# Attention in pairs of units, pinned on TensorE, with another order of branches, in a two-layer mixer step

## The chip, the cores and the metric

The kernel runs on one core of a Trainium2 chip. The metric is the device time of one execution in microseconds: the median of three runs, and beside it one execution that the hardware profiler recorded.

## What is computed

Two layers of a decoder step, for a prompt of 1024 tokens and 8 sample tokens (one new token for each of 8 sequences), model width 1024. Each layer projects the normalised input once and splits it among four branches of width 384, gates and projects them, merges them, and adds the result to the residual. Cut to what matters here:

```python
h = rms_norm(x, norm_g)
(a_b, a_c, a_h, a_gate, s_q, s_k, s_v, s_gate,
 c_u, c_v, c_gate, d_q, d_k, d_v, d_gate) = jnp.split(h @ w_in, SPLIT_POINTS, axis=-1)
y_a = a_b * conv3(a_c * a_h)                                    # A
o_b, _ = banded_window_attention(q, k, v, SWA_WINDOW, sink)     # B: 6 q heads, 2 kv heads, window 128
y_c = c_u * chunk_spatial_mix(vn, w_spatial, b_spatial)         # C
for g, (win, dil) in enumerate(((128, 1), (512, 4), (2048, 16))):
    o, lse = dilated_prompt_attention(qg, kg, vg, win, dil)     # D: 2 heads a group, blocks of 128
y_d = concat(o * softmax(lse over groups))
proj_b = einsum('bsne,ned->bsnd', [y_n * silu(gate_n)], w_branch)
x = x + sum(sigmoid(h @ w_merge) * proj_b) @ w_out
```

Attention works on blocks of 128 queries against at most 256 keys. The updated caches are outputs too.

## The kernel before, in words

Activations lie transposed in SBUF: 128 features on the partitions, 1032 token columns (8 sample tokens, then 1024). `slot` gives a tile of that size from a pool of 31. Every weight and every activation of a dense product is split into a high and a low fp32r part (`split_w`: ScalarE rounds to the high part, L154, GpSimd subtracts, L156), and a product is three matmuls for each 128 input features: high weight by high activation (L178), high by low (L181), low by high (L182), in chunks of 344 columns (`fm_tile`, `mm_cols`). The accumulators are `acc` tiles, one PSUM bank each. `tm_group` (L367 to L371) does the same with tokens on the partitions. These are called dense matmuls here.

Attention is cut into units: one block of 128 queries of two heads (one from each half of the partitions), against `nk` = 128 or 256 keys. Branch B has 24 units in a layer (8 blocks, 3 pairs of heads), branch D has 8 in each of 3 groups: 48 in a layer. For one unit, before:

- `scores` (L519): a matmul for each head, contraction over 64 partitions, into one `sc` bank each; VectorE scales, masks and takes the maximum (L521);
- `exps` (L527, ScalarE); in B the sum, its reciprocal and the scaling follow on VectorE (L568 to L576);
- `pv`: transpositions of the weights (L536) into an `ms` bank, a copy to SBUF on ScalarE (L538), and the matmuls with the values (L541) into another `ms` bank, which ScalarE copies out.

PSUM has 8 banks: 4 for `acc`, 2 for `sc`, 2 for `ms`.

The order on each engine isn't that of the source: a scheduler takes the instructions in the source's order of priority, by its own forecast of when each can start, and fills TensorE with whatever it holds to be ready. A few edges (`load`'s "prefetch distance") order DMAs behind matmuls. On the chip each engine keeps to the order built.

The branches come in this order: keys, queries and values of B; C's values; C's products, with B's units among them; then `conv_a(0, branch_d(0))`, decode of group 0 and of B, `gate_a(0)`, B's gates, `conv_a(1, branch_d(1))`, `gate_a(1)`, `conv_a(2, branch_d(2))`, the gate of group 0, the end of D's decode, `gate_a(2)`, and the merge. `branch_d(g)` projects and rotates one group's keys and queries (`rope`: a half swap by DMA, then VectorE and GpSimd, L289 to L297) and runs its 8 units. At the start `x` is transposed on TensorE (L259, L262) into `sc` and `ms` banks in turn, copied by VectorE (L264) and split (L207 to L214).

Of the kernel before, what the change touches and what calls it, by code (L numbers as in the profile page):

```python
# [7 lines left out]
F32 = mybir.dt.float32  # L8
F32R = mybir.dt.float32r
AF = mybir.ActivationFunctionType  # L10
ALU = mybir.AluOpType
# [21 lines left out]
def kernel(ctx: ExitStack, tc: tile.TileContext, i, o, c):  # L33
# [5 lines left out]
    sl = ctx.enter_context(tc.tile_pool(name="sl", bufs=31))  # L39
# [21 lines left out]
    def pscore():  # L61
        return psS.tile([P, 512], F32, tag="sc", name="sc")
# [188 lines left out]
    for n0, n1 in GROUPS:  # L251
# [22 lines left out]
    for l in range(2):  # L274
# [239 lines left out]
        def scores(qs, ks, nk, mask, mx):  # L514

            s = tp.tile([P, 2, 256], F32, tag="s", name="s", bufs=2)
            ps = [pscore() for _ in range(2)]
            for h in range(2):
                pe.matmul(ps[h][:, :nk], qs[h], ks[h], start=True, stop=True)  # L519
            for h in range(2):  # L520
                dve.tensor_tensor_reduce(s[:, h, :nk], ps[h][:, :nk], mask, scale=0.125,  # L521
                                         scalar=-3e38, op0=ALU.add, op1=ALU.max, accum_out=mx[:, h:h + 1])
            return s

        def exps(s, nk, negm, den):
            for h in range(2):
                act.activation(s[:, h, :nk], s[:, h, :nk], AF.Exp, bias=negm[:, h:h + 1],  # L527
                               accum_out=den[:, h:h + 1])

        def pv(s, nk, vs, out):  # L530

            kb = nk // P
            ps = pmisc()
            for h in range(2):
                for b in range(kb):
                    pe.transpose(ps[:, (h * kb + b) * P:(h * kb + b + 1) * P], s[:, h, b * P:(b + 1) * P], ident)  # L536
            pt = tp.tile([P, 512], F32, tag="pt", name="pt")
            act.activation(pt[:, :2 * nk], ps[:, :2 * nk], AF.Copy)  # L538
            for b in range(kb):
                for h in range(2):  # L540
                    pe.matmul(out[h * 64:(h + 1) * 64, :], vs[b][h], pt[:, (h * kb + b) * P:(h * kb + b + 1) * P],  # L541
                              start=(b == 0), stop=(b == kb - 1))
# [15 lines left out]
        stB = sm.tile([P, 8, 3, 4], F32, tag="stB", name="stB")  # L558
        for n in range(8):
# [3 lines left out]
            ks = halves(kB, (slice(None), kcols))  # L563
            for j in range(3):
                st = stB[:, n, j]
                s = scores(halves(qB[j], (slice(None), blkcols(n))), ks, nk, mask, st[:, 0:2])
                negm = st[:, 0:2]
                dve.scalar_tensor_tensor(negm, st[:, 0:2], -1.0, nsink[:, j], op0=ALU.mult, op1=ALU.min)  # L568
                exps(s, nk, negm, st[:, 2:4])
                es = sm.tile([P, 2], F32, tag="es", name="es", bufs=4)  # L570
                dve.tensor_tensor(es, negm, nsink[:, j], op=ALU.subtract)
                act.activation(es, es, AF.Exp)
                dve.tensor_tensor(es, es, st[:, 2:4], op=ALU.add)
                dve.reciprocal(es, es)
                for h in range(2):
                    dve.tensor_scalar(s[:, h, :nk], s[:, h, :nk], es[:, h:h + 1], None, op0=ALU.mult)  # L576
                kbs = (n - 1, n) if n else (n,)
                vs = [[vB[:, b, h * 64:(h + 1) * 64] for h in range(2)] for b in kbs]
                po = pmisc()
                pv(s, nk, vs, po[:, :P])  # L580
                act.activation(OB[j][:, blkcols(n)], po[:, :P], AF.Copy)
# [131 lines left out]
        def conv_a(j, rows):  # L713
# [7 lines left out]
            rows()  # L721
# [24 lines left out]
        def gate_a(j):  # L746
            y = yA[j]
            fm_tile(w_std(win_cols(l, A_B + P * j, P), KT), KT, hh, hl, ev_mul(y))
            fm_tile(w_std(win_cols(l, A_G + P * j, P), KT), KT, hh, hl, ev_silu(y))
            store_later(1, yscr[0][j], y)  # L750
# [4 lines left out]
        def branch_d(g):  # L755
# [8 lines left out]
            for nm, src, lst in (("dqs", dq, dqs), ("dks", dk, dks)):  # L764
                t = sm.tile([P, NS], F32, tag=f"{nm}{g}", name=f"{nm}{g}")
                dve.tensor_copy(t, src[:, 0:NS])
                lst.append(t)
            vg = load_v(1 + g)
# [3 lines left out]
            std = sm.tile([P, 8, 4], F32, tag="std", name="std")  # L772
            for u in range(8):
# [25 lines left out]
                s = scores(qv, kv_, nk, mask, std[:, u, 0:2])  # L799
                negm = sm.tile([P, 2], F32, tag="es", name="negm", bufs=4)  # L800
                dve.tensor_scalar(negm, std[:, u, 0:2], -1.0, None, op0=ALU.mult)
                exps(s, nk, negm, std[:, u, 2:4])
                po = pmisc()
# [273 lines left out]
```

## Time and profile before

| | |
|---|---|
| median of 3 runs | 2435.44 us (2435.28 to 2436.69) |
| the profiled execution, its own time | 2441.25 us |
| its span, first to last instruction | 2439.3 us |
| TensorE busy (matmul) | 2418.7 us, 99% |
| TensorE's weight loader busy | 2303.7 us, 94% |
| VectorE, ScalarE, GpSimd busy | 910.6, 703.4, 842.8 us |
| mean granted TensorE clock | 0.992 |
| chain that ended last | TensorE 95%, VectorE 2%, DMA 1%, ScalarE 1% |

TensorE has two rows: PE is matmuls, PEld is the loading of the stationary operand, which runs beside them. A matmul of two full fp32 operands (S and R here) appears as two records, a transposition or a dense fp32r matmul as one. A matmul's duration overlaps its successor's; the distance between two starts is what one costs.

### The profile page before, as it was taken

The page shows a single profiled execution, that of the slowest core. Times are in us where ns is not written, and L with a number is a line of the kernel's source. Part 1 is how long each engine was busy: PE and PEld are TensorE (multiplying, and loading weights), DVE is VectorE, ACT ScalarE, POOL GpSimd, SP SyncE. Part 2 cuts the span into 40 slices and gives each one's busy share as a digit, 9 for nine tenths or more (in the row PEclk, how much of TensorE's full clock was granted, in tenths as well). Part 3 has the DMA queues.
Part 4 walks back from the last instruction along what each step waited for, and adds up shares of the span by engine and source line. Part 5 has one row for each costly group of instructions (what it writes and reads, how often), then busy time and mean ns, then how long its engine had stood idle before and what let it go on. Part 6 is the DMA issues. An engine that isn't in the chain of part 4 may idle for free.

```text
span 2439.3 us, 38864 instructions
## 1 busy us (share of the span) xinstructions
PE 2418.7 (99%) x15896; PEld 2303.7 (94%) x15896; DVE 910.6 (37%) x1938; ACT 703.4 (29%) x1526; POOL 842.8 (35%) x556
## 2 busy tenths in 40 slices
PE   8999999999999999999999999999999999999999
PEld 7998889899999999999999888898999999999998
DVE  4456526354312221225323554443353221212253
ACT  6234432323212221214323253313222222222243
POOL 3342225342223343334433313342323234434330
PEclk9999999999899999999999999999999999999999
DMA  7252224343322222224443413242352222212232
GB/s 241 87 145 82 74 57 151 87 125 94 102 70 63 88 62 96 65 65 129 140 146 82 151 53 96 80 148 57 100 143 71 70 92 65 88 61 69 76 98 99
DMA packets 295962, 235.82 MB, mean 97 GB/s; under 512 B 52756, under 2 KB 279696, under 8 KB 293416
## 3 DMA queue, kind: packets, MB, share of 16 engines
q1 hardware_dynamic: 267952, 206.25, 28.1%
q10 hardware_dynamic: 27832, 27.10, 3.9%
q8 instruction: 125, 2.05, 0.4%
q14 instruction: 53, 0.43, 0.1%
HBM read 192.35 MB, written 76.47 MB: 110 GB/s over the span
## 4 chain that ended last, share of the span: by engine, by line
PE 95%; DVE 2%; DMA 1%; ACT 1%; ACTq 0%; issue 0%; POOL 0%; SPq 0%; DVEq 0%; POOLq 0%
PE acc L181 26%; PE acc L178 26%; PE acc L182 26%; PE sc L519 2%; PE acc L367 2%; PE acc L370 2%; PE acc L371 2%; PE ms L541 2%; PE ms L536 2%; PE ms L681 1%; DVE ml L901 0%; DMA wr<-in_w_in_dram 0%; PE ms L474 0%; ACT wh L154 0%; DMA qs<-dq 0%
## 5 line engine op out<-in xcount | busy, mean ns | idle before, releaser
L156 POOL TENSOR_TENSOR wl<-wr,wh 128x384 fp32r<-128x384 f32 (+2 forms) x228 | 462.7, 2031 | 925.5 <-ACT wh L154 796.8
L178 PE MATMUL acc<-h0h,wh 128*128 128x344 f32 x1584 | 513.4, 324 | 1.9 <-ACT wh L154 0.9
L178 PE MATMUL acc<-h1h,wh 128*128 128x344 f32 x1584 | 514.4, 325 | 0.9 <-ACT dk L281 0.5
L181 PE MATMUL acc<-h1l,wh 128*128 128x344 f32 x1584 | 513.5, 324 | 0.0
L181 PE MATMUL acc<-h0l,wh 128*128 128x344 f32 x1584 | 512.8, 324 | 0.0
L182 PE MATMUL acc<-h0h,wl 128*128 128x344 f32 x1584 | 512.5, 324 | 0.0
L182 PE MATMUL acc<-h1h,wl 128*128 128x344 f32 x1584 | 510.8, 323 | 0.0
L154 ACT ACTIVATE wh<-wr 128x384 fp32r<-128x384 f32 (+2 forms) x228 | 205.2, 901 | 457.4 <-PE acc L181 422.8
L936 DVE TENSOR_TENSOR th<-acc,rr 128x344 f32<-128x344 f32 x192 | 99.0, 516 | 565.9 <-PE acc L182 562.3
L181 PEld LDWEIGHTS acc<-h0l,wh 128*128 128x128 f32 x1584 | 300.3, 190 | 8.7 <-issue 7.6
L181 PEld LDWEIGHTS acc<-h1l,wh 128*128 128x128 f32 x1584 | 300.2, 190 | 8.3 <-issue 7.6
L178 PEld LDWEIGHTS acc<-h0h,wh 128*128 128x128 f32 x1584 | 300.1, 190 | 7.4 <-issue 2.7
L178 PEld LDWEIGHTS acc<-h1h,wh 128*128 128x128 f32 x1584 | 299.9, 189 | 5.8 <-issue 2.9
L182 PEld LDWEIGHTS acc<-h1h,wl 128*128 128x128 f32 x1584 | 300.4, 190 | 2.8 <-issue 1.8
L182 PEld LDWEIGHTS acc<-h0h,wl 128*128 128x128 f32 x1584 | 299.9, 189 | 2.8 <-issue 1.8
L942 POOL TENSOR_TENSOR mg<-mg,th 128x344 f32<-128x344 f32 x144 | 138.0, 958 | 308.4 <-DVE th L941 308.4
L937 ACT ACTIVATE th<-th 128x344 f32<-128x344 f32 x192 | 94.3, 491 | 520.9 <-DVE th L936 520.9
L178 PE MATMUL acc<-yh,wh 128*128 128x344 f32 x576 | 184.5, 320 | 0.0
L181 PE MATMUL acc<-yl,wh 128*128 128x344 f32 x576 | 184.0, 319 | 0.0
L182 PE MATMUL acc<-yh,wl 128*128 128x344 f32 x576 | 183.8, 319 | 0.0
L181 PE MATMUL acc<-ml,wh 128*128 128x344 f32 (+3 forms) x384 | 123.2, 322 | 0.5 <-DVE ml L901 0.5
L941 DVE SCALAR_TENSOR_TENSOR th<-th,acc 128x344 f32<-128x344 f32 x144 | 73.8, 512 | 130.2 <-PE acc L182 129.5
(280 smaller groups left out, 3363.9 us busy)
## 6 DMA issues: line engine op xcount, KB each, us to landing
wr<-in_w_merge_dram SPq DMA_DIRECT2D x64, 512.0 KB
out_dram<-in_cache_dil_kv_dram SPq DMA_DIRECT2D x128, 255.9 KB
wr<-in_w_in_dram SPq DMA_DIRECT2D x60, 512.0 KB
y<-yscr SPq DMA_DIRECT2D x18, 516.0 KB
wr<-in_w_branch_dram SPq DMA_DIRECT2D x48, 192.0 KB
wr<-in_w_in_dram SPq DMA_DIRECT2D x32, 256.0 KB
wr<-in_w_out_dram SPq DMA_DIRECT2D x16, 512.0 KB
out_dram<-in_cache_dil_kv_dram SPq DMA_DIRECT2D x16, 511.0 KB
```

Of the source, the lines that this page charges most:

```text
L154: act.activation(hi, raw, AF.Copy)
L156: pool.tensor_tensor(lo, raw, hi.bitcast(F32), op=ALU.subtract)
L178: mm = pe.matmul(ps[:, :n], hi[:, k], xh[k][:, cs], start=(k == 0), stop=False)
L181: pe.matmul(ps[:, :n], hi[:, k], xl[k][:, cs], start=False, stop=False)
L182: pe.matmul(ps[:, :n], lo[:, k], xh[k][:, cs], start=False, stop=(k == kt - 1))
L367: mm = pe.matmul(ps[:M, :N], lh, hi[:, k % kk], start=(k == 0), stop=False)
L370: pe.matmul(ps[:M, :N], ll, hi[:, k % kk], start=False, stop=False)
L371: pe.matmul(ps[:M, :N], lh, lo[:, k % kk], start=False, stop=(k == KT - 1))
L936: dve.tensor_tensor(t, pg[:, :CH], rr[:, cs], op=ALU.mult)
L937: act.activation(t, t, AF.Tanh, scale=0.5)
L941: dve.scalar_tensor_tensor(t, t, 1.0, pp[:, :CH], op0=ALU.add, op1=ALU.mult)
L942: pool.tensor_tensor(mg[m][:, cs], mg[m][:, cs], t, op=ALU.add)
```

## The change

The units of one attention are collected in a list, and `attend` works through them two at a time:

- `psS` becomes one tile of two banks, head by bank, which holds the scores of two units side by side; `psM` gets 3 banks, `psA` 3 instead of 4. Users of `sc` for other things take `acc` (input) or `ms` (final block).
- For a pair, the source issues on TensorE: its transpositions, then the results of the pair before, then the scores of the next pair. `pin` orders each of these behind the TensorE instruction that the source issued just before it (an order of issue, not a wait).
- `conv_a` no longer contains a branch D; `gate_a` is split into `in_a` (the product with A_B) and `out_a` (the gate); `branch_d` returns two functions, one for the cache rows and one for the attention, and the order of the calls changes.
- The pool of slots grows from 31 to 34.

```diff
-    sl = ctx.enter_context(tc.tile_pool(name="sl", bufs=31))
+    sl = ctx.enter_context(tc.tile_pool(name="sl", bufs=34))
...
-    psA = ctx.enter_context(tc.tile_pool(name="psA", bufs=4, space=bass.MemoryType.PSUM))
-    psS = ctx.enter_context(tc.tile_pool(name="psS", bufs=2, space=bass.MemoryType.PSUM))
-    psM = ctx.enter_context(tc.tile_pool(name="psM", bufs=2, space=bass.MemoryType.PSUM))
+    psA = ctx.enter_context(tc.tile_pool(name="psA", bufs=3, space=bass.MemoryType.PSUM))
+    psS = ctx.enter_context(tc.tile_pool(name="psS", bufs=1, space=bass.MemoryType.PSUM))
+    psM = ctx.enter_context(tc.tile_pool(name="psM", bufs=3, space=bass.MemoryType.PSUM))
...
-        return psS.tile([P, 512], F32, tag="sc", name="sc")
+        return psS.tile([P, 2, 512], F32, tag="sc", name="sc")
...
-            ps = pmisc() if k % 2 else pscore()
+            ps = pmisc() if k % 2 else pacc()
...
+        def attend(units):
+            pinned = [False]
+            def pin(ins):
+                if pinned[0]:
+                    tc.keep_in_program_order(ins)
+                pinned[0] = True
+            def scores(pair):
+                ps = pscore()
+                for a, u in enumerate(pair):
+                    for h in range(2):
+                        pin(pe.matmul(ps[:, h, a * 256:a * 256 + u.nk], u.qs[h], u.ks[h], start=True, stop=True))
+                return ps
...
+            def transposed(pair):
+                for u in reversed(pair):
+                    kb = u.nk // P
+                    ps = pmisc()
+                    for h in (1, 0):
+                        for b in range(kb):
+                            pin(pe.transpose(ps[:, (h * kb + b) * P:(h * kb + b + 1) * P],
+                                             u.s[:, h, b * P:(b + 1) * P], ident))
+                    u.pt = tp.tile([P, 512], F32, tag="pt", name="pt")
+                    act.activation(u.pt[:, :2 * u.nk], ps[:, :2 * u.nk], AF.Copy)
+            def results(pair):
+                po = pmisc()
+                for a, u in enumerate(pair):
+                    kb = u.nk // P
+                    for b in range(kb):
+                        for h in range(2):
+                            pin(pe.matmul(po[h * 64:(h + 1) * 64, a * P:(a + 1) * P], u.vs[b][h],
+                                          u.pt[:, (h * kb + b) * P:(h * kb + b + 1) * P],
+                                          start=(b == 0), stop=(b == kb - 1)))
+                for a, u in enumerate(pair):
+                    act.activation(u.out, po[:, a * P:(a + 1) * P], AF.Copy)
+            pairs = [units[n:n + 2] for n in range(0, len(units), 2)]
+            ps = scores(pairs[0])
+            for n, pair in enumerate(pairs):
+                soften(pair, ps)
+                pinned[0] = False
+                transposed(pair)
+                if n:
+                    results(pairs[n - 1])
+                if n + 1 < len(pairs):
+                    ps = scores(pairs[n + 1])
+            pinned[0] = False
+            results(pairs[-1])
...
         decD = Decode("D")
-        conv_a(0, branch_d(0))
+        rows, attention = branch_d(0)
+        conv_a(0, rows)
         decD.scores(0, dqs[0], dks[0])
+        attention()
+        in_a(0)
+        conv_a(1)
...
-        gate_a(0)
+        out_a(0)
...
-        conv_a(1, branch_d(1))
+        rows, attention = branch_d(1)
+        in_a(1)
+        rows()
         decD.scores(1, dqs[1], dks[1])
-        gate_a(1)
-        conv_a(2, branch_d(2))
+        attention()
+        out_a(1)
+        conv_a(2)
+        rows, attention = branch_d(2)
+        sg0 = gate_d(0)
+        rows()
         decD.scores(2, dqs[2], dks[2])
-        sg0 = gate_d(0)
+        attention()
+        in_a(2)
...
-        gate_a(2)
+        out_a(2)
```

`soften` holds the masked maximum of `scores` for both units and then each unit's softmax, unchanged in its operations.

How the built order moves, first on TensorE in B's attention of the first layer, in the middle of it. `v` are the values, `s` the weights, `kB` and `qB` keys and queries; the dense rows are C's products. Before:

```order
L178 MATMUL acc<-h0h_133,wh 128x344
L541 MATMUL ms<-pt,v_1753 64x128 x4
L536 MATMUL ms<-ident,s 128x128 x4
L519 MATMUL sc<-kB,qB_863 128x256 x2
L181 MATMUL acc<-h0l_141,wh 128x344
L182 MATMUL acc<-h0h_133,wl 128x344
```

And with the change:

```order
L178 MATMUL acc<-h0h_133,wh 128x344
L553 MATMUL ms<-ident,s 128x128 x8
L564 MATMUL ms<-pt,v_1753 64x128 x8
L535 MATMUL sc<-kB,qB_1242 128x256 x2
L535 MATMUL sc<-kB,qB_359 128x256 x2
L181 MATMUL acc<-h0l_141,wh 128x344
L182 MATMUL acc<-h0h_133,wl 128x344
```

The first kind of group stands after every 18 dense matmuls, the second after every 57 to 64, with twice the attention in it and the transpositions ahead.

Second on TensorE at the start of the program, where `xin` is the input that arrives by DMA. Before, dense matmuls stand among the transpositions from the 29th row on:

```order
L262 MATMUL sc<-ident,xin_97 128x128
L262 MATMUL sc<-ident,xin_101 128x128
L262 MATMUL sc<-ident,xin_103 128x128
L178 MATMUL acc<-h0h_128,wh 128x344
L181 MATMUL acc<-h0l_136,wh 128x344
L259 MATMUL ms<-ident,xs 128x8
L262 MATMUL ms<-ident,xin_97 128x128
```

With the change the first dense matmul is the 69th row, behind transpositions of the last two input blocks:

```order
L262 MATMUL acc<-ident,xin_120 128x128
L262 MATMUL acc<-ident,xin_122 128x128
L262 MATMUL ms<-ident,xin_120 128x128
L262 MATMUL ms<-ident,xin_122 128x128
L178 MATMUL acc<-h0h_128,wh 128x344
L181 MATMUL acc<-h0l_136,wh 128x344
```

The transpositions write `acc` and `ms` tiles there instead of `sc` and `ms`.

## Rows read from the trace of the kernel before

**Rows 1.** The page, its first part: busy us (share of the span) xinstructions by engine.

```profile
PE 2418.7 (99%) x15896; PEld 2303.7 (94%) x15896; DVE 910.6 (37%) x1938; ACT 703.4 (29%) x1526; POOL 842.8 (35%) x556
```

**Rows 2.** Waits of TensorE's matmuls: line, released by: us in total, times, longest.

```profile
PE sc L259 <- DMA xs<-in_x_sample_dram: 4.6, 1, 4.6
PE sc L519 <- DVE dqp L297: 3.6, 3, 3.2
PE ms L259 <- DVE xT L264: 2.4, 1, 2.4
```

**Rows 3.** Waits of TensorE's weight loader, same columns.

```profile
PEld ms L541 <- issue: 18.9, 87, 0.3
PEld sc L519 <- issue: 17.0, 91, 0.3
PEld acc L181 <- issue: 15.3, 48, 0.3
PEld ms L536 <- issue: 15.1, 88, 0.2
```

**Rows 4.** Timeline of TensorE in B's attention: start us, us, operation, xcount.

```profile
251.70 0.32 PE L182 MATMUL acc<-h0h,wl 128*128 128x344 f32 x1
251.85 0.32 PE L178 MATMUL acc<-h0h,wh 128*128 128x344 f32 x1
252.10 0.66 PE L541 MATMUL ms<-pt,v 128*64 128x128 f32 x8
252.69 0.66 PE L536 MATMUL ms<-ident,s 128*128 128x128 f32 x4
253.28 0.70 PE L519 MATMUL sc<-kB,qB 64*128 64x256 f32 x4
253.91 0.42 PE L181 MATMUL acc<-h0l,wh 128*128 128x344 f32 x1
254.17 0.32 PE L182 MATMUL acc<-h0h,wl 128*128 128x344 f32 x1
```

**Rows 5.** Timeline of TensorE near the end: transpositions among dense matmuls.

```profile
2415.61 0.34 PE L178 MATMUL acc<-mh,wh 128*128 128x384 f32 x1
2415.78 1.03 PE L973 MATMUL sc<-ident,xT 128*128 128x128 f32 x8
...
2416.84 0.35 PE L182 MATMUL acc<-mh,wl 128*128 128x384 f32 x1
```

**Rows 6.** Timeline of TensorE in D's first group: results of a short unit.

```profile
328.80 0.44 PE L541 MATMUL ms<-pt,v 128*64 128x128 f32 x4
```

**Rows 7.** Start: records on `acc` to 28.3 us by engine, and two dense starts.

```profile
0.00:28.30 28.30, 9.19 (x33) 6.70 (x34) 0.00 (x0) 0.00 (x0) 1.00 0.78 216
18.45 0.49 PE L178 MATMUL acc<-h0h,wh 128*128 128x344 f32 x1
18.74 0.49 PE L181 MATMUL acc<-h0l,wh 128*128 128x344 f32 x1
```

**Rows 8.** Timeline of VectorE at the start; in brackets its wait and what ended it.

```profile
8.46 0.57 DVE L264 COPY xT<-sc 128x392 f32<-128x392 f32 x1 [7.50 <-PE sc L262]
10.73 0.55 DVE L264 COPY xT<-sc 128x392 f32<-128x392 f32 x1
14.43 2.30 DVE L209 SCALAR_TENSOR_TENSOR h0l<-xT,gcol,h0h 128x392 fp32r<-128x392 f32 x1 [3.14 <-ACT h0h L207]
```

**Rows 9.** Timeline of VectorE in B's attention: the scaling of one unit's weights.

```profile
256.72 0.61 DVE L576 TENSOR_SCALAR s<-s,es 128x256 f32<-128x256 f32 x2
```

**Rows 10.** TensorE before a fall; stretches: us, PE busy (x), granted clock, DMA.

```profile
418.04 1.09 PE L681 MATMUL ms<-pd,cB 128*64 128x3 f32 x16
420.40:423.80 3.40, 3.40 (x14) 0.50 0.78 310
467.60:471.20 3.60, 3.60 (x21) 1.00 0.47 135
2430.90:2437.70 6.80, 3.08 (x26) 1.00 0.63 233
```

More of the change, by code (lines that the diff above doesn't have):

```diff
@@ L511, in cache_k @@
             act.dma_start(dst, kr)
-        def scores(qs, ks, nk, mask, mx):
-            s = tp.tile([P, 2, 256], F32, tag="s", name="s", bufs=2)
-            ps = [pscore() for _ in range(2)]
-            for h in range(2):
[L519 to L542, printed above, removed]
+        class Unit:
+            def __init__(self, qs, ks, nk, mask, vs, mx, den, soft, out):
+                self.qs, self.ks, self.nk, self.mask, self.vs = qs, ks, nk, mask, vs
+                self.mx, self.den, self.soft, self.out = mx, den, soft, out
@@ L544, in halves, with exps @@
+        def exps(u, negm):
+            for h in range(2):
+                act.activation(u.s[:, h, :u.nk], u.s[:, h, :u.nk], AF.Exp, bias=negm[:, h:h + 1],
+                               accum_out=u.den[:, h:h + 1])
         def halves(t, sel):
@@ L558 @@
         stB = sm.tile([P, 8, 3, 4], F32, tag="stB", name="stB")
+        units = []
         for n in range(8):
@@ L563, with soft @@
             ks = halves(kB, (slice(None), kcols))
+            kbs = (n - 1, n) if n else (n,)
+            vs = [[vB[:, b, h * 64:(h + 1) * 64] for h in range(2)] for b in kbs]
             for j in range(3):
-                st = stB[:, n, j]
[L566 to L581, printed above, removed]
+                def soft(u, j=j):
+                    negm = u.mx
+                    dve.scalar_tensor_tensor(negm, u.mx, -1.0, nsink[:, j], op0=ALU.mult, op1=ALU.min)
+                    exps(u, negm)
+                    es = sm.tile([P, 2], F32, tag="es", name="es", bufs=4)
+                    dve.tensor_tensor(es, negm, nsink[:, j], op=ALU.subtract)
+                    act.activation(es, es, AF.Exp)
+                    dve.tensor_tensor(es, es, u.den, op=ALU.add)
+                    dve.reciprocal(es, es)
+                    for h in range(2):
+                        dve.tensor_scalar(u.s[:, h, :u.nk], u.s[:, h, :u.nk], es[:, h:h + 1], None, op0=ALU.mult)
+                st = stB[:, n, j]
+                units.append(Unit(halves(qB[j], (slice(None), blkcols(n))), ks, nk, mask, vs, st[:, 0:2], st[:, 2:4],
+                                  soft, OB[j][:, blkcols(n)]))
+        attend(units)
         class Decode:
@@ L711, with conv_a @@
         yA = [None] * 3
-        def conv_a(j, rows):
+        def conv_a(j, rows=None):
             y, z = slot(f"yA{j}"), slot("z")
@@ L720, in conv_a @@
             fm_tile(w_std(win_cols(l, A_C + P * j, P), KT), KT, hh, hl, ev_copy)
-            rows()
+            if rows:
+                rows()
             pool.tensor_tensor(z, z, rr, op=ALU.mult)
@@ L772, in branch_d, with soft @@
             std = sm.tile([P, 8, 4], F32, tag="std", name="std")
+            units = []
+            def soft(u):
+                negm = sm.tile([P, 2], F32, tag="es", name="negm", bufs=4)
+                dve.tensor_scalar(negm, u.mx, -1.0, None, op0=ALU.mult)
+                exps(u, negm)
             for u in range(8):
@@ L798, in branch_d @@
                     oview = og[:, NS:].rearrange("p (i u) -> p u i", u=8)[:, u]
[L799 to L803, printed above, removed]
-                pv(s, nk, vs, po[:, :P])
-                act.activation(oview, po[:, :P], AF.Copy)
+                units.append(Unit(qv, kv_, nk, mask, vs, std[:, u, 0:2], std[:, u, 2:4], soft, oview))
+            attend(units)
             if g == 0:
@@ L840 @@
             store_later(1, yscr[1][j], OB[j])
-        conv_a(1, branch_d(1))
+        rows, attention = branch_d(1)
+        in_a(1)
+        rows()
         decD.scores(1, dqs[1], dks[1])
-        gate_a(1)
-        conv_a(2, branch_d(2))
+        attention()
[3 more added lines that the diff above has]
+        sg0 = gate_d(0)
+        rows()
         decD.scores(2, dqs[2], dks[2])
-        sg0 = gate_d(0)
+        attention()
+        in_a(2)
         values_d = decD.finish(OD)
```

20 lines of the change are left out of this document (15 added, 5 removed).

## Prediction

> **What bounds the kernel now.** I read the page first: TensorE is busy for 2418.7 of 2439.3 us [rows 1]. The list of what TensorE waited for shows how little of the rest has a name: 4.6 us for the first input, 3.6 us for a rotated query, 2.4 us at the start, and 1.0 us or less in each later row [rows 2]. So faster work on other engines shortens nothing here; only TensorE's own stream can. Its matmuls fall into two kinds: the dense ones (L178, L181, L182 and the token-major L367 to L371), and those of attention: transpositions T (L536), results R (L541), scores S (L519). The third view asks why the weight loader stood still, although TensorE counts as busy then. The word is "issue": 18.9 us in 87 times ahead of R, 17.0 us in 91 times ahead of S, 15.1 us in 88 times ahead of T, 15.3 us in 48 times ahead of the dense L181 [rows 3]: 66 us, some 0.2 each time that the stream goes from one kind to another.
>
> **The price of one visit to attention.** I call a run of other matmuls between two dense ones a visit. The commonest is R, T, S of three units in flight [rows 4]. Dense starts lie 0.157 us apart. Then: dense to R 0.25 us, R 0.59, T 0.59, S 0.63, and the first dense one after it 0.26. From 251.85 to 254.17 that is 2.32 us, or 2.01 more than the two dense matmuls in it.
>
> What of that is work? A dense matmul at 2415.61 is followed by eight transpositions 0.17 us later, and the second dense one after them starts 1.06 us after the first transposition; without one dense pitch of 0.17 that is 0.89, 0.11 for each T [rows 5]. So going into T and out of it is free: it has the dense matmuls' shape, 128*128, while R runs as 128*64 and S as 64*128. R with 8 records lasts 0.66 us and with 4 records 0.44 [rows 4, 6], so 4 records cost 0.22. The S of one unit I keep at 0.63. A unit of 256 keys then has 0.44 + 0.44 + 0.63 = 1.51 us of work in its visit, and 0.50 us goes to changes of kind.
>
> **The change, part by part.** *Pairs.* A full visit now holds 8 T, 8 R (16 records) and 4 S. T first: entry 0, work 0.87. T to R is a change that no row shows; between 0 and 0.25 (dense to R with its first start), I take 0.14: 0.09 by which dense to R exceeds a dense pitch, and 0.05 for R's slower first block. R 0.88. R to S, not shown either: between 0 and 0.2 (a stop of the loader), I take 0.10, what R to T costs now (0.59 for 0.44 of work, less the 0.05). S 1.26, and 0.11 on the first dense one after it. Together 3.36 us for two units against 2 x 2.01 = 4.02: 0.66 less.
>
> Not every visit is full. I counted them in both built orders, both layers together. Before there are 154 visits with attention in them (44 full ones; others hold S alone, 24 times, or R and T alone). In the timeline the first of them lies at 123.6 us, the last at 1777 us; the 146 with nothing else cost 176 us above their dense matmuls, the 44 full ones 88 us of it, and the attention in the other 8 some 5 us. The change has 64, of which 18 hold 8 T, 8 R and 4 S and 20 are nearly so. The work is the same in both: 320 T at 0.11, 320 R at 0.11, 64 units with S of 0.63 and 32 units of 128 keys with S of 0.42, 124 us. So changes of kind cost 181 - 124 = 57 us now, 0.37 a visit. In the new order each visit, priced by its parts as above, has 0.33 of them, 21 us in all. **The gain is 36 us.** Its ends: 27 us, if the 66 us of [rows 3] shrink only as the changes of kind in the built order do, 725 to 428; and 45 us, if each of the 90 visits saved is worth 0.50.
>
> *Other work* (decode, convolution, cache rows) has its own visits, 107 before and 84 now, with the same matmuls: between 0 and 3 us of gain, I take 0.
>
> *The start.* The input's transpositions now share psA with the dense accumulators. Before, 33 dense matmuls have started by 28.3 us [rows 7]. In the new order 68 of 72 transpositions stand ahead of the first dense one, and it needs an accumulator that VectorE's 17th copy frees; ahead of that copy stand 16 others and 8 splits. These are 25 instructions of some 0.5 us, 12 us from the first at 8.46 [rows 8], so 20 us without a wait. VectorE waited 3.1 us in one place of this stretch before; I take 24 (bounds 20 and 28). At the start the dense pitch is 0.29 [rows 7], so 15 start between 24 and 28.3. The missing 18 cost 18 x 0.157 = 3 us. Ends: 0, since the transpositions now have 6 buffers instead of 4, and 7.
>
> *Buffers.* Dense accumulators go from 4 to 3. A chunk takes 24 x 0.157 = 3.8 us and its reader about 0.5, so two chunks of slack remain: nothing. Where gate and product alternate (24 and 9 matmuls), an accumulator is wanted again after 5.2 us by a chain of three steps of 0.5: nothing. Both banks of scores are read by VectorE well before the next visit: nothing, unless the first rival is right. *Three more slots, another order of branches:* the first scores of a dilated group wait for rotated queries, 3.6 us in 3 times, 3.2 of it once [rows 2]. By the built orders the TensorE work between a group's last query product and its first scores is 12.5 us in all three groups before, and now 34 us in the first, 12.7 and 12.3 in the others. So this wait may vanish or come again: 0, with 7 us (two such waits) either way.
>
> **Sum.** 36 - 3 = 33 us off the profiled execution's 2441.25 us: 2408. The median of the runs is 2435.44, 5.8 us below that execution, so I predict **2402 us**.
>
> **Rivals.**
> *A new wait: T waits for softmax.* T of a pair stands one visit after its S. One unit's S starts at 253.28 and its scaled scores are done at 257.33, 4.1 us [rows 4, 9]; two units take between 4.1 and 8.2, more where the readers of dense chunks cut in. The new order puts 55 to 64 dense matmuls (8.6 to 10 us) there in the B branch, and 38 to 47 (6.0 to 7.4) in D, where a unit lacks the scaling. So the slack is thin in D: if its 24 pairs waited 1 us each, 24 us of the gain would be gone: 2426; at half of that, 2414.
> *Slower: the clock falls after long visits.* A full visit grows from 2.0 to 3.4 us without a dense matmul. If the granted clock fell to 1.2 GHz after such a visit, each fall would cost half of its length: from 420.4 to 423.8, where 14 matmuls ran at 0.50, 1.7 us [rows 10]. The 33 us are gone at 20 falls; if all 38 full or nearly full visits caused one, 65 us would be lost: 2467. For it: that fall came straight after 2 us of decode's narrow matmuls (L681) [rows 10], so not everything on TensorE holds the clock. Against it: from 467.6 to 471.2, with 2.2 us of S, R, T, S in one piece, it stayed at 1.00 (2.4 GHz), and so it did from 2430.9 to 2437.7, where little but transpositions ran, for 3.08 of 6.8 us [rows 10].
> The Trainium skill speaks for this rival: "TensorE: Matmul & The Clock Gate", section "Part 4: PE-mode transpose", says that transpositions do not count as busy in the way that matmuls do, so a visit that opens with eight of them would sooner lower the clock. By that rule the sum would lose what this rival loses; the last stretch of [rows 10] does not bear it out.
> *The change does not do what it says.* A pin orders a matmul behind the one before it and does not forbid dense ones in between. The built order shows whole visits, so the mechanism could fail only in its prices: with T to R at 0.25 and R to S at 0.2 in some 40 and 32 visits, 8 us come back: 2410.
>
> **How the numbers follow.** The gain arrives as forecast, with the ends of its terms (2435 less 45 and 7: 2384; 2435 less 27, plus 7 at the start or in waits: 2415): 0.78. Waits or dearer changes eat a third or more of it (2410 to 2430): 0.12. The clock falls: 0.10, in most of that so often that it ends slower. The range takes the first case from its lower end and reaches to 2428, for most of the second. Less than 0.2% (4.9 us) a measurement cannot tell from no change. Faster by more: 0.88; within: 0.04; slower: 0.08.
>
> **What would show it.** Right: the loader's "issue" time ahead of T, R, S and L181 falls from 66 to about 35 us; a full visit takes 3.3 to 3.5 us; TensorE's named waits stay under 20 us; the first dense matmul starts near 24 us. Wrong: the line of T among TensorE's waits with 10 us or more, a mean clock under 0.98, or full visits beyond 3.7 us.

## The result, and the profile after

The changed kernel takes 2405.0 us (median of 4 runs, 2401.8 to 2412.4) against 2436.0 us for the kernel before (4 runs): ratio 0.9877, 95% interval [0.9854, 0.9900]. Forecast were 2402 us and a range of 2384 to 2428. The profiled execution took 2405.88 us, its span is 2404.1 us, its mean granted clock 0.990 (0.992 before).

The page's first part, and TensorE's largest waits (line, released by: us in total, times, longest):

```profile
PE 2372.6 (99%) x15896; PEld 2309.2 (96%) x15896; DVE 888.1 (37%) x1938; ACT 687.7 (29%) x1522; POOL 845.3 (35%) x556
```

```profile
PE ms L553 <- DVE s L622: 5.3, 3, 2.5
PE acc L178 <- DVE yA L746: 4.7, 2, 2.4
...
PE ms L553 <- ACT pt L556: 2.0, 2, 1.3
```

TensorE still does nearly all the work [rows 1] and is busy 46 us less. But its named waits have grown, from 15.9 us over all rows to 27.6: transpositions (L553) wait for scaled weights, dense matmuls for the readers of their accumulators (yA). The wait of 3.2 us for rotated queries [rows 2] has not come back. The weight loader's stops of unknown cause ("issue") shrank as they should, from 66 us ahead of T, R, S and L181 [rows 3] to 29; the 6.0 us ahead of T, in three stops of up to 2.8 us, are its waits for weights seen from the loader, so 23 us are left for changes of kind:

```profile
PEld acc L181 <- issue: 8.0, 26, 0.3
PEld sc L535 <- issue: 7.9, 43, 0.3
PEld ms L564 <- issue: 7.2, 40, 0.3
PEld ms L553 <- issue: 6.0, 3, 2.8
```

A full visit, in TensorE's timeline (start us, us, operation, xcount); it answers to [rows 4]:

```profile
240.45 0.32 PE L181 MATMUL acc<-h0l,wh 128*128 128x344 f32 x1
240.60 1.04 PE L553 MATMUL ms<-ident,s 128*128 128x128 f32 x8
241.57 1.09 PE L564 MATMUL ms<-pt,v 128*64 128x128 f32 x16
242.59 1.13 PE L535 MATMUL sc<-kB,qB 64*128 64x256 f32 x8
243.66 0.43 PE L182 MATMUL acc<-h0h,wl 128*128 128x344 f32 x1
243.92 0.32 PE L178 MATMUL acc<-h0h,wh 128*128 128x344 f32 x1
```

From 240.45 to 243.92 that is 3.47 us, 3.16 more than two dense pitches of 0.157; forecast were 3.36. Going into T is free, as the old trace had promised (0.15 from the dense start to T). T with its change to R takes 0.97 (forecast 1.01), R with its change to S 1.02 (0.98), the exit 0.10 (0.11). S is the one that was off: 1.07 instead of 1.26. One unit's S costs 0.63, a second one behind it only 0.44.

Not all visits are that clean. At 304.8 us T waits; TensorE, then VectorE (in brackets the wait and what ended it), then stretches (us, busy us of PE, PEld, DVE, ACT and POOL, granted clock, DMA):

```profile
304.81 0.32 PE L178 MATMUL acc<-h0h,wh 128*128 128x344 f32 x1
307.67 0.66 PE L553 MATMUL ms<-ident,s 128*128 128x128 f32 x2 [2.55 <-DVE s L622]
```

```profile
300.73 3.49 DVE L290 TENSOR_TENSOR dq<-dq,cosT 128x1032 f32<-128x1032 f32 x1 [4.13 <-DMA qs<-dq]
304.13 0.15 DVE L614 SCALAR_TENSOR_TENSOR stB<-stB,nsink 128x2 f32<-128x2 f32 x1
...
306.39 1.14 DVE L622 TENSOR_SCALAR s<-s,es 128x256 f32<-128x256 f32 x4
```

```profile
304.80:307.40 2.60, 0.32 (x3) 0.04 (x1) 2.60 (x12) 0.80 (x6) 0.00 (x0) 1.00 0.00 0
307.40:310.80 3.40, 3.13 (x20) 2.83 (x22) 0.55 (x2) 0.03 (x1) 0.00 (x0) 0.50 0.00 0
```

In VectorE's queue the multiplication of `rope` stands ahead of the softmax of the last pair of B, and it waits 4.13 us for the half swap by DMA. The weights come late, T waits 2.55 us, and from the end of that wait the clock is at 0.50 (1.2 GHz) for 3.4 us. Something like it happens at 348 and 1526 us, where a dense matmul waits 2.2 and 2.4 us for an accumulator whose reader (yA, L746) stands behind a late convolution:

```profile
350.08 0.66 PE L178 MATMUL acc<-h0h,wh 128*128 128x344 f32 x1 [2.21 <-DVE yA L746]
```

and the stretch at 0.50 there, columns as above:

```profile
348.40:355.20 6.80, 5.12 (x18) 5.12 (x19) 2.47 (x11) 2.08 (x8) 3.08 (x2) 0.50 0.76 223
```

This stretch begins 0.5 us into that wait, behind two shorter ones (0.7 and 0.8 us). At 1526 us the clock falls 0.2 us ahead of the wait of 2.4 us, behind waits of 1.3 and 0.7 us, and stays at 0.50 for 6.8 us too.

The start was dearer than forecast: the first dense matmul starts at 27.97 us; in the kernel before, 33 records on accumulators had started by 28.3 us [rows 7].

```profile
27.97 0.63 PE L178 MATMUL acc<-h0h,wh 128*128 128x344 f32 x1 [0.94 <-DVE xT L264]
```

### The profile page after: what moved, and what is told of

Same layout as the page of the kernel before. It is cut to its first block, busy times and chain, and to the rows that moved or that the text cites. A ratio compares the mean times of both kernels' runs of the same rounds, so it can differ in the third digit from the quotient of the medians.

```text
span 2404.1 us, 38761 instructions
## 1 busy us (share of the span) xinstructions
PE 2372.6 (99%) x15896; PEld 2309.2 (96%) x15896; DVE 888.1 (37%) x1938; ACT 687.7 (29%) x1522; POOL 845.3 (35%) x556
## 4 chain that ended last, share of the span: by engine, by line
PE 95%; DVE 2%; DMA 1%; ACT 0%; issue 0%; SPq 0%; POOL 0%; ACTq 0%; DVEq 0%; POOLq 0%
PE acc L181 27%; PE acc L182 27%; PE acc L178 27%; PE acc L367 2%; PE acc L371 2%; PE acc L370 2%; PE ms L564 2%; PE sc L535 2%; PE ms L553 2%; PE ms L726 1%; PE ms L474 0%; DMA qs<-dq 0%; PE ms L1035 0%; DMA wr<-in_w_in_dram 0%; DVE xT L264 0%
## 5 line engine op out<-in xcount | busy, mean ns | idle before, releaser
L156 POOL TENSOR_TENSOR wl<-wr,wh 128x384 fp32r<-128x384 f32 (+2 forms) x228 | 476.5, 2092 | 855.4 <-ACT wh L154 764.4
L181 PE MATMUL acc<-h1l,wh 128*128 128x344 f32 x1584 | 511.3, 323 | 0.0
L181 PE MATMUL acc<-h0l,wh 128*128 128x344 f32 x1584 | 510.9, 323 | 0.0
L181 PEld LDWEIGHTS acc<-h0l,wh 128*128 128x128 f32 x1584 | 300.5, 190 | 4.6 <-issue 4.0
L181 PEld LDWEIGHTS acc<-h1l,wh 128*128 128x128 f32 x1584 | 300.1, 189 | 4.6 <-issue 4.0
L181 PE MATMUL acc<-yl,wh 128*128 128x344 f32 x576 | 184.3, 320 | 0.0
L181 PE MATMUL acc<-ml,wh 128*128 128x344 f32 (+3 forms) x384 | 123.1, 321 | 0.0
L182 PE MATMUL acc<-mh,wl 128*128 128x344 f32 (+3 forms) x384 | 122.9, 320 | 0.0
```

The lines of the kernel that those rows point to most:

```text
L156: pool.tensor_tensor(lo, raw, hi.bitcast(F32), op=ALU.subtract)
L181: pe.matmul(ps[:, :n], hi[:, k], xl[k][:, cs], start=False, stop=False)
L182: pe.matmul(ps[:, :n], lo[:, k], xh[k][:, cs], start=False, stop=(k == kt - 1))
```

## Experiments

The theory: fewer changes of kind on TensorE make the gain, and waits and the start give part of it back. The rivals: the other order of branches makes it; the pins make it; long visits cost clock. All runs in one table; "waits" is the sum of the waits named for TensorE's matmuls, "clock" the mean granted clock, both of the profiled execution. The kernel before had medians of 2436.0 to 2437.8 us beside them. "Order" is that of the branches, "banks" accumulators + `ms`. The four runs of the change lie 10.6 us apart, so differences of a few us from it are not told apart. The expectations count 686 changes of kind before and 386 in the change where the prediction counts 725 and 428; how the two counts differ is not on record.

| run | groups | order | pins | banks | median us | ratio to before | waits us | clock |
|---|---|---|---|---|---|---|---|---|
| before | 1 | old | no | 4+2 | 2436.0 | 1 | 15.9 | 0.992 |
| the change | 2 | new | yes | 3+3 | 2405.0 | 0.9877 [0.9854, 0.9900] | 27.6 | 0.990 |
| e1_single | 1 | new | yes | 3+3 | 2545.4 | 1.0442 [1.0419, 1.0464] | 109.6 | 0.966 |
| e2_nopin | 2 | new | no | 3+3 | 2391.3 | 0.9813 [0.9793, 0.9833] | 17.4 | 0.995 |
| e3_old_order | 2 | old | yes | 3+3 | 2462.5 | 1.0103 [1.0085, 1.0121] | 69.7 | 0.982 |
| e4_start_banks | 2 | new | yes | 3+3 | 2404.2 | 0.9862 [0.9841, 0.9883] | 27.8 | 0.991 |
| e5_single_nopin | 1 | new | no | 3+3 | 2428.1 | 0.9969 [0.9960, 0.9979] | 17.7 | 0.994 |
| e6_old_order_nopin | 2 | old | no | 3+3 | 2428.5 | 0.9972 [0.9962, 0.9981] | 42.2 | 0.988 |
| e7_two_ahead | 2 | new | yes | 3+3 | 2388.0 | 0.9804 [0.9790, 0.9817] | 18.8 | 0.996 |
| e8_nopin_start | 2 | new | no | 3+3 | 2391.6 | 0.9820 [0.9807, 0.9833] | 15.8 | 0.995 |
| e9_single_old_nopin | 1 | old | no | 3+3 | 2466.7 | 1.0124 [1.0110, 1.0137] | 50.3 | 0.987 |
| e10_two_ahead_start | 2 | new | yes | 3+3 | 2391.3 | 0.9814 [0.9800, 0.9827] | 19.2 | 0.997 |
| e11_transpose_twice | 2 | new | yes | 3+3 | 2427.9 | 0.9966 [0.9954, 0.9979] | 22.2 | 0.996 |
| e12_single_old_four_acc | 1 | old | no | 4+2 | 2447.8 | 1.0053 [1.0040, 1.0067] | 29.7 | 0.990 |

**e1_single: pairs undone, pins kept.**

```diff
-            pairs = [units[n:n + 2] for n in range(0, len(units), 2)]
+            pairs = [units[n:n + 1] for n in range(len(units))]
```

> The changed kernel with groups of one unit instead of two: transpositions of one unit, results of the one before, scores of the next, still pinned, same order of branches, same PSUM. The built order has 92 visits with attention instead of 64 and 536 changes of kind on TensorE instead of 386. Theory (changes of kind set the time): 150 changes at about 0.1 us each, 15 us, and the loads of the second unit's scores, hidden in a pair, show again, 0.1 us for each of some 96 units, 9 us: 20 to 28 us slower than the changed kernel, 2425 to 2433. Rival (the new order of the branches and the three more slots did it, pairs are neutral): within 5 us of the changed kernel.

Measured: 140 us slower than the change. Neither side had that; it is no price of changes but waits, 54.7 us of them in 17 of the 92 visits, and the clock behind them (0.966). TensorE's largest wait, and its timeline in B:

```profile
PE ms L553 <- DVE s L622: 54.7, 17, 4.4
```

```profile
341.87 1.09 PE L553 MATMUL ms<-ident,s 128*128 128x128 f32 x4 [3.43 <-DVE s L622]
...
343.94 1.23 PE L535 MATMUL sc<-kB,qB 64*128 64x256 f32 x4
348.60 1.09 PE L553 MATMUL ms<-ident,s 128*128 128x128 f32 x4 [3.43 <-DVE s L622]
```

A pin puts the next scores behind the transpositions. So S, softmax and T follow each other strictly, 6.7 us a turn here, and this order was built with seven visits and nothing in between. From 320 to 420 us (columns as above) TensorE works 68.5 us, at a mean granted clock of 0.69:

```profile
320.00:420.00 100.00, 68.50 (x395) 53.04 (x392) 33.08 (x133) 30.34 (x99) 11.85 (x6) 0.69 0.16 43
```

**e2_nopin: pins taken away.**

```diff
                 if pinned[0]:
-                    tc.keep_in_program_order(ins)
+                    pass
```

> The changed kernel without the pins, pairs kept: the scheduler may take scores apart from transpositions and results. The built order has 104 visits with attention instead of 64, and 432 changes of kind instead of 386. Theory (changes of kind): 46 changes at 0.1 us, and an extra half scores-to-dense penalty at each of 40 lone visits, 0.1 us: 5 to 9 us slower than the changed kernel, 2410 to 2414. Rival (the pins are what the gain rests on): most of the 31 us gone, 2425 or more. Other rival (without pins the scores come earlier, so that transpositions no longer wait for the softmax, 7 us of waits): same or faster than the changed kernel.

Measured: 14 us faster than the change; the other rival holds. The built order puts 40 S runs on their own, ahead of the transpositions of the pair before; the long waits of T (0.7 us left) and for yA are gone, and with them the clock falls there. The price is small. A visit of T and R alone takes 2.41 us from dense start to the second dense start, one of S alone some 1.6:

```profile
228.95 0.33 PE L181 MATMUL acc<-h0l,wh 128*128 128x344 f32 x1
229.11 1.03 PE L553 MATMUL ms<-ident,s 128*128 128x128 f32 x8
230.08 1.09 PE L564 MATMUL ms<-pt,v 128*64 128x128 f32 x16
231.10 0.42 PE L182 MATMUL acc<-h0h,wl 128*128 128x344 f32 x1
```

**e3_old_order: the old order of branches, pairs and pins kept.**

```diff
         rows, attention = branch_d(0)
+        attention()
         conv_a(0, rows)
         decD.scores(0, dqs[0], dks[0])
-        attention()
-        in_a(0)
-        conv_a(1)
...
         decB.finish(OB)(0)
+        in_a(0)
         out_a(0)
```

(groups 1 and 2 likewise)

> The changed kernel with the branches called in the order of the kernel before (each dilated attention inside its own conv_a place, in_a directly ahead of out_a); pairs, pins, PSUM and 34 slots kept. The built order has 54 visits with attention instead of 64, 342 changes of kind instead of 386. Theory (changes of kind): 44 changes at 0.1 us less, 4 us faster than the changed kernel, 2398 to 2403, if no new wait comes; the wait for rotated queries (3.2 us before) may return. Rival (the order of branches made the gain): 2420 or more, with named waits of TensorE well above 28 us.

Measured: 57 us slower than the change, with the fewest changes of kind of all. The rival holds: counting changes says nothing once waits decide.

```profile
PE ms L553 <- ACT s L585: 19.1, 6, 3.9
PE ms L660 <- DVE qr L651: 13.8, 8, 4.4
PE acc L178 <- DVE yA L746: 5.7, 6, 2.0
```

**e4_start_banks: the start's transpositions off the accumulators.**

```diff
-            ps = pmisc() if k % 2 else pacc()
+            ps = pmisc() if k % 4 else pscore()[:, 0]
```

> The changed kernel, but the transpositions of the input at the start use the three ms banks and one sc bank, not the accumulators of the dense products; the first dense matmul stands behind 28 transpositions again instead of 68. Theory (the shared accumulators cost the start): first dense matmul near 18 us instead of 28, 30 or so dense matmuls by 28.3 us, 5 to 7 us faster than the changed kernel, 2398 to 2400. Rival (VectorE's copies and splits set the start, banks do not matter): first dense matmul earlier, but the stream waits for the split parts, gain under 2 us.

Measured: the same time as the change within the scatter (2398.9 to 2409.9). TensorE's records by 45 and by 70 us, in the kernel before, the change and this run:

```profile
0.00:45.00 45.00, 36.79 (x204) 1.00 0.83 254
0.00:70.00 70.00, 61.79 (x409) 1.00 0.73 225
```

```profile
0.00:45.00 45.00, 34.12 (x169) 0.96 0.89 275
0.00:70.00 70.00, 57.63 (x349) 0.98 0.74 224
```

```profile
0.00:45.00 45.00, 35.50 (x192) 1.00 0.86 250
0.00:70.00 70.00, 57.71 (x351) 0.98 0.75 224
```

By 45 us it has won 23 of the 35 records lost, by 70 us 2 of 60. The row norms (L328) lie between: VectorE starts on the reciprocals they need at 54.1 us here (50.7 in the change), since the sums of squares come later in ScalarE's queue. TensorE then waits twice for 1.0 us between 60.5 and 63.1 us, and the granted clock is at 0.50 from 63.2 to 66.6 us. The change has a slow stretch of that length at 27.5 us instead. It is a gain handed back some 20 us further on.

**e5_single_nopin: pairs undone, no pins.**

```diff
-                    tc.keep_in_program_order(ins)
+                    pass
...
-            pairs = [units[n:n + 2] for n in range(0, len(units), 2)]
+            pairs = [units[n:n + 1] for n in range(len(units))]
```

> Groups of one unit and no pins, all else as in the changed kernel; to be compared with the pairs without pins (2391 us). The built order has 184 visits with attention instead of 104 and 652 changes of kind on TensorE instead of 432. Theory (pairs are worth their changes of kind, and the pinned groups of one lost 140 us by waits alone): 220 changes at 0.1 us, 22 us, and up to 9 us for the loads of the second unit's scores that a pair hides: 2413 to 2422, and TensorE's named waits under 30 us. Rival (pairs gain nothing by themselves, the order of branches does): within 5 us of 2391.

Measured: 36.8 us slower than the pairs of e2, at equal waits and clock; 6 us beyond the range. So pairs by themselves are worth 37 us here. Spread over 220 changes of kind that is 0.17 us each, the second unit's hidden loads included.

**e6_old_order_nopin: old order of branches, pairs, no pins.** The calls stand as in e3, and

```diff
-                    tc.keep_in_program_order(ins)
+                    pass
```

> Pairs without pins, branches called in the order of the kernel before. The built order has 102 visits and 390 changes of kind, against 104 and 432 with the new order. Theory (the 58 us that the old order cost beside pins are waits for the softmax that only pins make): no such waits, and 42 changes at 0.1 us fewer, 2385 to 2392. Rival (the old order has too little other work around the dilated attention, with pins or without): T or the decode lines wait over 10 us, 2400 or more.

Measured: 37 us slower than e2. T no longer waits, but the rival holds: decode (L660) and its neighbours do, as in e3.

```profile
PE ms L660 <- DVE qr L651: 11.9, 8, 4.0
PE acc L178 <- DVE yA L746: 3.6, 6, 1.3
```

**e7_two_ahead: pins kept, scores two pairs ahead.**

```diff
-            ps = scores(pairs[0])
+            soften(pairs[0], scores(pairs[0]))
+            pinned[0] = False
+            soften(pairs[1], scores(pairs[1]))
             for n, pair in enumerate(pairs):
-                soften(pair, ps)
...
-                if n + 1 < len(pairs):
-                    ps = scores(pairs[n + 1])
+                if n + 2 < len(pairs):
+                    soften(pairs[n + 2], scores(pairs[n + 2]))
```

and `bufs=4` for the tile `s`.

> The changed kernel with its pins, but the scores are issued two pairs ahead of their transpositions instead of one (four buffers of s instead of two). 86 visits with attention, 426 changes of kind, against 64 and 386. Theory (a pin puts the next scores behind the transpositions, so the whole softmax has to fit between two visits; with one more pair in flight it does): T's waits fall from 7.3 us to under 2, the clock falls behind them go, 4 us for 40 more changes: 2392 to 2398. Rival (long visits without dense matmuls are what costs, by the clock, and not waits): no better than 2405.

Measured: 2388.0 us, 17 us faster than the change and the fastest of all. No T wait is left in the list. What is named in attention now is S, for the bank that VectorE still reads, and one load of values:

```profile
PE sc L535 <- DVE std L542: 2.7, 4, 0.9
...
PE ms L564 <- DMA v<-vscr: 1.2, 1, 1.2
```

Of the 17 us, 9 are named waits (27.6 to 18.8), and the clock's loss, one minus its mean times the span, falls from 24 to 9 us. The two overlap where a wait lies in a slow stretch, and 40 more changes of kind take some 4 back (an estimate at 0.1 us each). Of the clock's 15 us, 8.5 belong to the falls at the waits that are gone (17 us at 0.50) and 7 to decode, behind whose narrow matmuls the clock is at 0.50 for 27.3 us in the change and for 13.7 here; why that is less here no run shows.

**e8_nopin_start: e2 and e4 together.**

```diff
-            ps = pmisc() if k % 2 else pacc()
+            ps = pmisc() if k % 4 else pscore()[:, 0]
...
-                    tc.keep_in_program_order(ins)
+                    pass
```

> Pairs without pins, and the start's transpositions on the ms and sc banks. Theory (the start's 5 us come back at the row norms, L328, whose chain on ScalarE and VectorE ends at 51 to 54 us whatever TensorE did before): TensorE is 5 us ahead at 45 us and level again at 65 us, 2388 to 2392. Rival (that loss was an accident of one built order): 2384 to 2387.

Measured: as e2. At 45 us TensorE has 192 records (e2 160), at 70 us 355 (e2 338), and its 410th record starts 2.0 us earlier than in e2: much of the lead is gone by then, with the clock at 0.50 from 63.2 us as in e4, and the rest does not show in the time.

**e9_single_old_nopin: groups of one, old order, no pins.** The calls stand as in e3, and

```diff
-                    tc.keep_in_program_order(ins)
+                    pass
...
-            pairs = [units[n:n + 2] for n in range(0, len(units), 2)]
+            pairs = [units[n:n + 1] for n in range(len(units))]
```

> Groups of one, no pins, old order of branches: what is left of the change is T ahead of R, the new split of the PSUM banks, the start on the accumulators and 34 slots. 178 visits with attention, 612 changes of kind on TensorE (the kernel before: 154 and 686). Theory (pairs and order of branches together make the gain, the banks only cost the start): 7 us lost at the start, 74 fewer changes at 0.1 us: 2436 to 2443. Rival (banks and slots carry part of the gain): under 2430.

Measured: 30 us slower than the kernel before; both expectations missed, in the same direction. Decode and convolution are built in larger pieces (some 70 visits of other work instead of some 105), and wait inside them:

```profile
PE ms L660 <- DVE qr L651: 13.6, 8, 4.1
PE acc L178 <- DVE yA L746: 5.7, 6, 2.0
```

**e12_single_old_four_acc: e9 with four accumulators and two `ms` banks.**

```diff
-tc.tile_pool(name="psA", bufs=3, space=bass.MemoryType.PSUM)
+tc.tile_pool(name="psA", bufs=4, space=bass.MemoryType.PSUM)
...
-tc.tile_pool(name="psM", bufs=3, space=bass.MemoryType.PSUM)
+tc.tile_pool(name="psM", bufs=2, space=bass.MemoryType.PSUM)
```

> Groups of one, no pins, old order (2467 us), with four accumulator banks and two ms banks as in the kernel before; sc stays one tile of two banks, slots stay 34, T still stands ahead of R. 100 visits of other work in the built order, against 71 with three and three banks and 107 in the kernel before. Theory (the 30 us are the price of the banks: with three accumulators the dense work cannot run on beside decode and convolution, which are then built in one piece and wait for VectorE): the waits of L660 and of the accumulators for yA fall from 19 to under 5 us, 2436 to 2446. Rival (the order in which a unit's steps are issued costs it): 2455 or more.

Measured: 18.9 of the 30 us are back, just outside the range; L660 and yA have left the list of waits, and waits for the readers of gates come first:

```profile
PE acc L178 <- DVE g L875: 5.1, 2, 2.8
```

So the split of the banks costs 19 us in this order. Of the 12 us left, 9 have arisen by 70 us (TensorE's 410th record starts 9.3 us later than before).

**e10_two_ahead_start: e7 and e4, and four of nine sums of squares on VectorE.**

```diff
+        if n % 2:
+            dve.tensor_tensor_reduce(junk2[:M, :DM], src[:M, :DM], src[:M, :DM], scale=1.0, scalar=0.0, op0=ALU.mult, op1=ALU.add, accum_out=sq0[:M, n:n + 1])
+        else:
             act.activation(junk[:M, :DM], src[:M, :DM], AF.Square, accum_out=sq0[:M, n:n + 1])
```

> Scores two pairs ahead, pinned (2388 us), and in addition the start's transpositions on the ms and sc banks and four of the nine sums of squares for the row norms on VectorE instead of ScalarE, which had worked on them until 52 us while VectorE idled. Theory (what gave the start's gain back was the end of the chain of squares on ScalarE): the reciprocal norms are ready before 50 us, TensorE stays about 5 us ahead of the two-ahead kernel at 70 us: 2381 to 2384. Rival (another wait takes its place): 2387 or more.

Measured: no faster than e7. The reciprocals start at 47.4 us (50.7 in the change), as wanted, but the squares took their turn in VectorE's queue ahead of the split parts, for which dense matmuls now wait (VectorE, then TensorE's waits):

```profile
28.71 1.21 DVE L273 CUSTOM_DVE_ANT_0 junk<-xin 128x1024 f32<-128x1024 f32 x1
...
29.86 2.75 DVE L209 SCALAR_TENSOR_TENSOR h0l<-xT,gcol,h0h 128x384 fp32r<-128x384 f32 x1
```

```profile
PE acc L181 <- DVE h0l L209: 3.5, 2, 3.0
```

After that wait the clock is at 0.50 from 41.2 to 44.6 us. By 70 us it has 351 records, e7 347. The start's loss moved three times and never left: each of these starts has one stretch of 3.4 us at 0.50 (27.5 us in the change, 63.2 in e4 and e8, 41.2 here), and the kernel before has none from 21 us, where its record of the clock begins, to 420 us.

**e11_transpose_twice: e7 with every T issued twice into the same place.**

```diff
-                            pin(pe.transpose(ps[:, (h * kb + b) * P:(h * kb + b + 1) * P],
-                                             u.s[:, h, b * P:(b + 1) * P], ident))
+                            for again in range(2):
+                                pin(pe.transpose(ps[:, (h * kb + b) * P:(h * kb + b + 1) * P],
+                                                 u.s[:, h, b * P:(b + 1) * P], ident))
```

> Scores two pairs ahead, pinned (2388 us), with each transposition of the weights issued twice into the same place: 320 more of them, and a full visit grows from 3.2 to 4.1 us. Theory (visits cost their work and never the clock; the falls come after waits): 320 at 0.11 us, 35 us: 2420 to 2426, mean clock 0.993 or above, no more falls than before. Rival (long stretches of transpositions and narrow matmuls lower the clock): mean clock under 0.985 and 2435 or more.

Measured: 39.8 us slower than e7, at the same clock (0.996). A visit of 4.1 us without a dense matmul, and the granted clock around it:

```profile
1423.20 1.91 PE L554 MATMUL ms<-ident,s 128*128 128x128 f32 x16
1425.04 1.09 PE L565 MATMUL ms<-pt,v 128*64 128x128 f32 x16
1426.06 1.14 PE L535 MATMUL sc<-kB,qB 64*128 64x256 f32 x8
1427.12 0.43 PE L178 MATMUL acc<-h1h,wh 128*128 128x344 f32 x1
```

```profile
1420.00:1440.00 20.00, 20.00 (x173) 17.45 (x170) 12.74 (x64) 12.83 (x46) 2.38 (x1) 1.00 0.02 6
```

Eight T more cost 0.87 us (T ahead of R 1.84 instead of 0.97), 0.11 each: 35 of the 39.8. The rival fails for attention: e11 and e7 have five falls each, none of them behind T, R and S.

## Why the prediction was right

The time came out 3 us from the forecast, in its range and for the case held likeliest. By steps:

- **Pairs, 36 us forecast.** Right in mechanism, and too small in size. With order, banks and lack of pins held equal, pairs are worth 36.8 us in the new order (e5 to e2) and 38.2 in the old (e9 to e6). That these meet the 36 is partly luck: their groups of one have T ahead of R already, while the forecast's term held both, pairs and T first. Counted in the forecast's own way from the two timelines (visits with attention alone, above their dense matmuls, waits and slow clock taken off), 146 visits cost 177 us before and 54 cost 123 us in the change. With the attention in the other visits at the prediction's prices, that is about 180 and 133: an estimate of 47 us, above the upper end of 45. T first has a share in it: the 158 such visits of e12 cost 164 us. Within a visit only S was mis-sized (1.26 forecast, 1.07 measured), and issue time without T's waits fell to 23 us, not 35.
- **"Dense accumulators go from 4 to 3 ... nothing", and the start at 3 us.** Wrong. Banks, start, T ahead of R and slots (and `dynamic_dma_scratch_size=1024`, which the change also sets for the program) together cost 30 us in the old order (before to e9), 19 of it through three accumulators and three `ms` banks. The forecast counted how long an accumulator is held by dense work alone; it did not ask what the builder of the order does with decode and convolution when it has one accumulator less. The start costs some 7 us by 70 us in the change, not 3: the first dense matmul came at 28 us, the upper bound.
- **"Another order of branches ... 0, with 7 us either way".** Wrong: 38.6 us in groups of one (e9 to e5), 37.2 in pairs (e6 to e2), with the new banks. The old order leaves decode and convolution too little other work beside them, by the named waits (42.2 us in e6, 17.4 in e2) and the clock (0.988, 0.995). With the old banks the new order was not tried.
- **Pins at nothing.** Wrong: 13.7 us (e2 to the change). The rival "T waits for softmax" named this mechanism, expected it in D, and bounded it at 24 us. It came at few places, mostly at the end of B, where `rope` holds VectorE's queue, and part of its cost is the clock after the wait.
- Hence the sum: 2436.4, plus 30.3 for the banks and start, less 38.6 for the order, less 36.8 for pairs, plus 13.7 for pins: 2405.0. The three terms beside the pairs add up to 5 (forecast 3): that the time came out this close is luck, three misses that cancel. This chain adds up by construction, and each term holds for the step at which it was taken. The two profiled executions alone tell it more shortly: 47 us won in the visits, 12 given back in named waits and 5 to the clock (20 us lost before, 24 now), which leaves 30 of the 35 us between them.
- **Rival of the clock.** No fall came behind a visit of T, R and S that had no wait in it; e11 settles that. The falls that the change adds lie at waits, 17 us at 0.50 in three places. But the larger part, 27 of 49 us at 0.50, lies behind decode's narrow matmuls (L726, one or three columns, with L724 between) without any wait, in the change as in the kernel before (31 of 39 us; [rows 10] has one of them). Columns as above:

```profile
610.20:614.60 4.40, 4.40 (x67) 4.28 (x67) 2.88 (x2) 0.00 (x0) 1.62 (x1) 1.00 1.13 212
614.60:624.90 10.30, 10.30 (x62) 10.21 (x62) 5.96 (x9) 2.62 (x3) 2.27 (x1) 0.50 1.04 288
```

So a long visit can lower the clock, though attention's did not. The prediction's last stretch against this rival was misread: the row ends at 2437.7 us just where the clock fell to 0.50, behind 2.7 us without work, so it says nothing on transpositions. The rule of the Trainium skill ("TensorE: Matmul & The Clock Gate", "Part 4: PE-mode transpose"), that transpositions do not count as busy in the way that matmuls do, would have had the clock fall in e11 first of all; it stayed at 1.00. That is between dense matmuls; no run here has a long stretch of transpositions alone.

- **What would show it.** T's line stayed under 10 us (7.3) and the clock above 0.98, as stated. A full visit took 3.2 us (forecast 3.3 to 3.5), the first dense matmul came at 28.0 us (24), and named waits were 27.6 us, not under 20; that miss pointed at the 17 us that e7 still found.

## What to carry to other kernels

Cost a rearrangement by more than the engine's own steps: an order that ties S behind T ties the whole softmax between two visits, and with one group more in flight the tied kernel gained 17 us and was as fast as the one without pins (2388.0 against 2391.3 us). A term set to zero because "two chunks of slack remain" needs a look at who else shares the buffers and at what the order then puts in one piece. And a lead won ahead of a join (the row norms here) is only kept if the other branch of the join comes earlier too, and in e10 not even then; test it by counting records at two times, not by the first instruction that starts sooner.

## What was not expected of the hardware

- A second unit's scores cost 0.44 us where the first cost 0.63. The loader's stops ahead of S come 43 times in the change and 91 times before [rows 3], about once a run and not once a matmul; that the other loads run beside matmuls is a reading of these numbers, not tried by itself.
- The place of T matters, and not only the count of changes: with T behind a dense matmul, a single unit's visit takes 1.91 us from dense start to dense start (e5, from 277.66 to 279.57), with R there instead 2.06 [rows 4].
- A wait can cost twice. With 2.55 us without work the granted clock went to 0.50 for 3.4 us, and among the waits around 348 us for 6.8 us; in e1, where waits came one after the other, it was 0.69 on average over 100 us. A wait of 1.27 us at 290.6 us in the change had no fall behind it.
- A busy TensorE can lose its clock too: behind 4.4 us of decode's narrow matmuls, busy throughout by its records, it was at 0.50 for 10.3 us.
